# Moving work across the seam between w_out and the MLP of a transformer block

## The chip, the cores and the metric

The kernel runs on one core of a Trainium2 chip, as one launch. The metric is the device time of the whole launch in microseconds (us), the median of several runs; lower is better.

## The reference

One transformer block in float32, for 512 tokens and a width of 2048. A first half mixes two attentions (`nsa_attention` and `retention`) and projects the mix with `w_out`; a second half is an MLP of width 8192 with a squared relu. Each half is normalised before and after:

```
mix = concatenate([o_a, o_r], axis=-1) @ w_out[l]      # (512, 2048) @ (2048, 2048)
x = x + rms_norm(mix, norm_mix_post[l])
h = rms_norm(x, norm_mlp_pre[l])
u = square(relu(h @ w_up[l]))                          # (512, 2048) @ (2048, 8192)
x = x + rms_norm(u @ w_down[l], norm_mlp_post[l])      # (512, 8192) @ (8192, 2048)
```

## The kernel before, in words

**Splits.** Every float32 operand of a matmul is split into a high part (a cast to fp32r on ScalarE: `whi`, `Hh`) and a low part (the rest, a subtract on VectorE: `wlo`, `Hl`). A product of two such operands is three matmuls into the same PSUM tile, high by high, low by high, high by low (`mm3`, L154 to L156). So each piece of weight costs a load from HBM (asked for by SyncE), a cast, a subtract, and then matmuls. The tiles `whi` and `wlo` of the MLP lie in a pool of three buffers each, `hilo`.

**w_out.** Its 2048 columns are done in four blocks of 416 and a last block of 384 ("ends"). The first four are driven slab by slab (a slab is 256 rows of weight) by `drv.run`. The eight slabs of the last block, `wend[0..7]`, are loaded, cast and subtracted in a loop that alternates with the last steps of the fourth block: a step, then a slab's load. Their raw and split tiles lie in space that is given back at the end of this part. The last block then goes token tile by token tile: four tiles of 128 tokens, each 8 slabs x 6 matmuls. When a tile's columns are done, `mix_done` squares and sums them on ScalarE (L823) and scales them into `Y` on VectorE (L824).

**From w_out to the MLP.** Per token tile t, `x1_chain(t)` forms the norm's factor (a `pow` on GpSimd, L161), adds the residual `x` quarter by quarter (VectorE L1002; the x tile comes from HBM by `x_fetch`, and the next tile's quarter is asked for as soon as this one's is used), squares it on ScalarE (L1005), stores it (L1009) and forms the second norm's factor. `x1_out(t)` scales `Y` into `xh` (ScalarE L1022), transposes it on TensorE into the PSUM tile `PT` (L1035), multiplies by the gain back into `Y` (VectorE L1037) and splits it into `Hh`, `Hl` (`halves`: L143 and L144). Both are generators, cut into pieces by `yield`. `norm_pieces(t)` weaves the pieces of the chain of tile t with those of the output of tile t−1 in a written order. `beside(mainly, every, work)` takes a piece of `work` after every so many steps of the matmuls of `mainly`. The last tiles' pieces, and the sums of row quarters that the MLP needs (`x1_sums`, L1052 and L1060), are taken beside the first MLP products by `work3`, with a rate `due`.

**The up projection.** It works in 16 blocks of 512 hidden columns with a Strassen-like scheme of seven products (p = 0 to 6) per block, each with its own sum of weight quarters (11, 12, 21, 22) and sum of activation quarters. A product has two slabs of 24 matmuls of 128x256. `ADD` says which quarter is added to which (L949 on VectorE, or for product 3 by a DMA from GpSimd that accumulates on the way in, `late_sum`, L916), `SPLIT` which quarter is then split. Products 0 and 1 of blocks 0 to 3 and product 0 of block 4 need only the first two token tiles; they are done first ("early"). Then the blocks follow as 0, 4, 1, 5, 2, 6, 3, 7, 8 and so on, each in the order (0, 1, 2, 5, 4, 3, 6) of what is left. Blocks 1, 2 and 3 so have five products.

`up_done` combines the products into hidden values after each one; its tail after product 6 is four sums on VectorE (L1180 to L1183).

**Feed.** The class `Feed` runs ahead of the matmuls: `load` asks for a 1 MB quarter (two slabs) on SyncE (L923) whenever a slot is free, `advance` does a slab's add and cast (L949, L953) and then the subtract of the slab before it (`low`, L929); it keeps three slabs ahead. A slot comes free when the last subtract that reads its quarter has been issued. The slots are two parts of `low`, three lent tiles `pre` and later two rows of `Y`; the third part of `low` holds x. Each engine runs its own instructions strictly in program order.

Of the kernel before, what the change touches and what calls it, by code (L numbers as in the profile page):

```python
# [10 lines left out]
F32 = mybir.dt.float32  # L11
# [5 lines left out]
P = 128  # L17
S = 512
# [94 lines left out]
def block_kernel(ctx: ExitStack, tc: tile.TileContext, x, norm_mix_pre, w_in, cmp_pe_k, cmp_w1_k, cmp_b1_k,  # L113
# [738 lines left out]
    wend = slabs_of(w_out, [(NB * WB, LAST)], pool_r)  # L852
    for s in range(NSLAB):
        drv.run(16 * B + s + 1)
        wend[s].load()
    wctx.close()
# [11 lines left out]
    ptp = ctx.enter_context(tc.tile_pool(name="ptp", bufs=2, space=PS, side="right"))  # L868
    pr0 = ctx.enter_context(tc.tile_pool(name="pr0", bufs=1, space=PS, side="right"))
    hp = ctx.enter_context(tc.tile_pool(name="hilo", bufs=3, side="right", reuse_waits="tile"))  # L870
    rw = ctx.enter_context(tc.tile_pool(name="raws", bufs=1, side="right", reuse_waits="tile"))
    low = rw.tile([P, 6144], F32, name="low")
    xh = mp.tile([P, 2048], F32, name="xh")
# [12 lines left out]
    class Feed:  # L886
# [4 lines left out]

        def __init__(self, phases, slots, ahead):
            self.phases, self.free, self.ahead, self.lent = phases, list(slots), ahead, []
            self.n, self.at, self.R, self.ready = 0, 0, {}, {}
            self.loads, self.last = [], {}
            for i, (g, prod, source) in enumerate(phases):
                for q in (SPLIT[prod],) if self.by_dma(i) else (ADD[prod] or ()) + (SPLIT[prod],):
                    if (g, q) not in self.last:
                        self.loads.append((g, q, source, i))
                    self.last[g, q] = i  # L900
            self.held = None

        def by_dma(self, i):

            g, prod, _ = self.phases[i]
            return prod == 3

# [9 lines left out]

        def load(self):
            while self.loads and self.free and self.loads[0][3] <= self.n // 2 + self.ahead:
                g, q, source, _ = self.loads.pop(0)  # L920
# [18 lines left out]
        def advance(self):  # L939
# [10 lines left out]
            src = self.R[g, SPLIT[prod]][:, c]  # L950
            hi = hp.tile([P, SL], F32R, name="whi")
            lo = hp.tile([P, SL], F32R, name="wlo")
            nc.scalar.copy(hi, src)  # L953
# [33 lines left out]

    xt = [low[:, c:c + 512] for c in range(4096, 6144, 512)]

# [24 lines left out]
    def x1_out(t):  # L1014
# [16 lines left out]
        for q in range(4):  # L1031
# [6 lines left out]
            scaled(q + 2)  # L1038
            if q == 1 and t < 2:
                halves(0)  # L1040
            if q == 3:
                halves(8)
            yield

    def x1_sums(pair):
# [33 lines left out]

    def norm_pieces(t):  # L1080

        c = x1_chain(t) if t < NT else iter(())
        o = x1_out(t - 1) if t else iter(())
        for work in (o, o, o, o, o, c, c, c, c) if t == 2 else (c, o, c, c, o, o, c, o, o):
            if next(work, "end") != "end":
                yield
# [15 lines left out]
    phases = [((b, p), p, up_source(b)) for b, p in early]  # L1102
    phases += [(b, p, up_source(b)) for b in blocks for p in ORDER if (b, p) not in early]
    nup = len(phases)
# [9 lines left out]
    phases += [(("down", c, nb), p, dn_source(c, nb)) for c in range(NCH) for nb in range(2) for p in ORDER]  # L1114
    feed = Feed(phases, [low[:, 0:2048], low[:, 2048:4096]], 3)
    x5 = mp.tile([P, 512], F32, name="x5")
    tmp = Ring(*xt, *(xh[:, c:c + 512] for c in range(0, 2048, 512)), x5)
    state = [{} for _ in range(NBLK)]
# [8 lines left out]
    def up_done(b, p, ps):  # L1127
# [9 lines left out]
        if p == 0:  # L1137
            z["p0"] = tmp.take()
            nc.scalar.copy(v2(z["p0"]), ps)
# [4 lines left out]
        elif p == 2:  # L1144
            if b == 0:
                tmp.views = [Y[:, t, c:c + 512] for t in (1, 3) for c in range(0, 2048, 512)]
            elif b == NPRO:
                tmp.views += xt[:2]
            elif b == NPRO + 1:
                tmp.views += xt[2:] + [x5]  # L1150
            z["v"] = tmp.take()
# [59 lines left out]
    def primed():  # L1211
        for _ in range(2):
            feed.advance()
            yield

    for q in range(4):
        x_fetch(0, q)
    beside(ends[0][1](), 3, primed())
    beside(ends[1][1](), 1, norm_pieces(0))
    beside(ends[2][1](), 1, norm_pieces(1))  # L1220
    beside(ends[3][1](), 1, norm_pieces(2))
    rsctx.close()
# [3 lines left out]
    pr1 = ctx.enter_context(tc.tile_pool(name="pr1", bufs=2, space=PS))  # L1226
    pools = (pr1, pr0, pr1)
    sxv = [sxp.tile([P, 8, 2 * P], F32R, name=f"sx{i}") for i in range(2)]
    prctx = ExitStack()
    prp = prctx.enter_context(tc.tile_pool(name="prim", bufs=1, reuse_waits="tile"))  # L1230
    feed.lent = [prp.tile([P, 2048], F32, name=f"pre{i}") for i in range(3)]
    feed.free += feed.lent
    XA = [tuple(H[:, 0:8, 0:256] for H in (Hh, Hl)), tuple(H[:, 8:16, 0:256] for H in (Hh, Hl)),
# [21 lines left out]
    def work3():  # L1255
        yield from norm_pieces(3)
        yield from both(x1_sums(0), norm_pieces(4))
        feed.free += [Y[:, 0, :], Y[:, 2, :]]
        yield from x1_sums(1)
# [3 lines left out]
    for n, _ in enumerate(up(0, len(early), pools, XA)):  # L1263
        due += 1 if n < 9 else 0.6
        while due >= 1:
# [18 lines left out]

    g4 = low[:, 4096:6144]

# [132 lines left out]
```

## Time and profile before

| | us |
|---|---|
| runs shown, median (lowest to highest) | 2258.95 (2256.57 to 2261.75) |
| the profiled execution | 2263.74 |
| its span, first to last instruction | 2261.9 |
| TensorE busy | 2175.6 |
| VectorE busy | 1563.7 |
| ScalarE busy | 986.9 |
| mean granted TensorE clock | 0.989 |

w_out's last block starts at 900.32 us of the span, the MLP's first product at 946.98, and the down projection follows the up projection at about 1590. The page divides the span into 40 slices; a stage is read from the windows and timelines of that stage, not from the means over the span.

### The profile page before, as it was taken

The page shows a single profiled execution, that of the slowest core. Times are in us where ns is not written, and L with a number is a line of the kernel's source. Part 1 is how long each engine was busy: PE and PEld are TensorE (multiplying, and loading weights), DVE is VectorE, ACT ScalarE, POOL GpSimd, SP SyncE. Part 2 cuts the span into 40 slices and gives each one's busy share as a digit, 9 for nine tenths or more (in the row PEclk, how much of TensorE's full clock was granted, in tenths as well). Part 3 has the DMA queues.
Part 4 walks back from the last instruction along what each step waited for, and adds up shares of the span by engine and source line. Part 5 has one row for each costly group of instructions (what it writes and reads, how often), then busy time and mean ns, then how long its engine had stood idle before and what let it go on. Part 6 is the DMA issues. An engine that isn't in the chain of part 4 may idle for free.

```text
span 2261.9 us, 31774 instructions
## 1 busy us (share of the span) xinstructions
PE 2175.6 (96%) x12787; PEld 1919.0 (85%) x12787; DVE 1563.7 (69%) x1868; ACT 986.9 (44%) x1432; POOL 129.1 (6%) x147
## 2 busy tenths in 40 slices
PE   8999999999999999889999999999899999999994
PEld 7888878878787999889999999999778888888873
DVE  6223556554656623587777878787778998899897
ACT  5213343342232323564554555555654444444442
POOL 0000000000000000100000000000000000000002
PEclk9999999999999999999999999999999999999997
DMA  6543224322324334675876767666665656566655
GB/s 191 140 118 91 79 73 95 90 75 87 89 70 145 95 106 127 205 213 169 223 204 178 203 168 206 168 208 187 202 208 160 212 159 214 152 205 165 192 144 83
DMA packets 251989, 344.76 MB, mean 152 GB/s; under 512 B 14107, under 2 KB 163947, under 8 KB 251201
## 3 DMA queue, kind: packets, MB, share of 16 engines
q1 hardware_dynamic: 212000, 288.23, 39.4%
q0 software_dynamic: 29744, 42.96, 12.0%
q10 hardware_dynamic: 10098, 11.55, 1.5%
q8 instruction: 100, 1.64, 0.3%
q14 instruction: 47, 0.39, 0.1%
HBM read 300.95 MB, written 41.75 MB: 152 GB/s over the span
## 4 chain that ended last, share of the span: by engine, by line
PE 77%; DVE 12%; DMA 4%; ACT 3%; issue 3%; POOL 1%; SPq 0%; ACTq 0%; POOLq 0%; DVEq 0%
PE prod L155 13%; PE prod L156 13%; PE prod L154 13%; PE mm L154 11%; PE mm L156 10%; PE mm L155 10%; DVE wlo L929 4%; DMA Y<-in_w_up 2%; DVE Hl L144 2%; PE S L583 2%; ACT whi L953 1%; DVE low L949 1%; DVE Y L949 1%; DVE acc L1315 1%; DMA low<-in_w_up 1%
## 5 line engine op out<-in xcount | busy, mean ns | idle before, releaser
L953 ACT CAST whi<-Y 128x1024 fp32r<-128x1024 f32 x228 | 238.4, 1049 | 305.8 <-DVE Y L949 119.0
L155 PE MATMUL prod<-wlo,Hh 128*128 128x512 f32 x896 | 352.3, 393 | 18.3 <-DVE wlo L929 18.3
L156 PE MATMUL prod<-whi,Hl 128*128 128x512 f32 x896 | 349.0, 390 | 0.0
L154 PE MATMUL prod<-whi,Hh 128*128 128x512 f32 x896 | 348.7, 389 | 0.0
L953 ACT CAST whi<-low 128x1024 fp32r<-128x1024 f32 x214 | 224.3, 1052 | 282.2 <-DVE low L949 105.9
L144 DVE TENSOR_TENSOR wlo<-raw,whi 128x1024 fp32r<-128x1024 f32 (+4 forms) x152 | 168.6, 1113 | 255.9 <-ACT whi L143 255.4
L929 DVE TENSOR_TENSOR wlo<-Y,whi 128x1024 fp32r<-128x1024 f32 x228 | 277.6, 1222 | 61.6 <-ACT whi L953 59.9
L929 DVE TENSOR_TENSOR wlo<-low,whi 128x1024 fp32r<-128x1024 f32 x214 | 260.8, 1222 | 54.4 <-ACT whi L953 52.7
L156 PE MATMUL prod<-Hh,wlo 128*128 128x256 f32 x1024 | 286.2, 279 | 11.2 <-DVE wlo L929 11.2
L154 PE MATMUL prod<-Hh,whi 128*128 128x256 f32 x1024 | 285.7, 279 | 5.1 <-DVE Y L824 5.1
L155 PE MATMUL prod<-Hl,whi 128*128 128x256 f32 x1024 | 284.7, 278 | 0.0
L143 ACT CAST whi<-raw 128x1024 fp32r<-128x1024 f32 (+4 forms) x152 | 145.4, 960 | 302.5 <-PE mm L155 147.9
L154 PE MATMUL mm<-whi,Hh 128*128 128x416 f32 (+4 forms) x704 | 263.3, 374 | 0.5 <-ACT Hh L143 0.4
L156 PE MATMUL mm<-whi,Hl 128*128 128x416 f32 (+4 forms) x704 | 248.6, 353 | 0.6 <-DVE Hl L144 0.5
L155 PE MATMUL mm<-wlo,Hh 128*128 128x416 f32 (+4 forms) x704 | 248.1, 352 | 0.0
L155 PEld LDWEIGHTS prod<-wlo,Hh 128*128 128x128 f32 x896 | 168.1, 188 | 65.5 <-DVE wlo L929 31.0
L156 PE MATMUL prod<-sx,wlo 128*128 128x256 f32 x768 | 215.1, 280 | 8.1 <-DVE wlo L929 8.1
L154 PE MATMUL prod<-sx,whi 128*128 128x256 f32 x768 | 214.7, 280 | 0.5 <-ACT whi L953 0.5
L154 PE MATMUL mm<-Hh,whi 128*128 128x512 f32 x512 | 214.7, 419 | 0.1
L155 PE MATMUL prod<-sx,whi 128*128 128x256 f32 x768 | 214.5, 279 | 0.0
L156 PEld LDWEIGHTS prod<-Hh,wlo 128*128 128x128 f32 x1024 | 194.3, 190 | 13.6 <-DVE wlo L929 13.4
L156 PE MATMUL mm<-Hh,wlo 128*128 128x512 f32 x512 | 200.5, 392 | 0.0
(289 smaller groups left out, 3970.4 us busy)
## 6 DMA issues: line engine op xcount, KB each, us to landing
raw<-in_w_in SPq DMA_DIRECT2D x160, 256.0 KB, 3.1
low<-in_w_up SPq DMA_DIRECT2D x38, 1024.0 KB, 6.2
Y<-in_w_up SPq DMA_DIRECT2D x32, 1024.0 KB, 6.1
low<-in_w_down SPq DMA_DIRECT2D x32, 1024.0 KB, 5.2
Y<-in_w_down SPq DMA_DIRECT2D x32, 1024.0 KB, 5.2
Y<-ud SPq DMA_DIRECT2D x49, 512.0 KB, 8.4
ud<-Y SPq DMA_DIRECT2D x73, 256.0 KB, 4.7
raw<-in_w_out SPq DMA_DIRECT2D x32, 416.0 KB, 3.5
```

Of the source, the lines that this page charges most:

```text
L143: nc.scalar.copy(hi, src)
L144: nc.vector.tensor_sub(lo, src, hi.bitcast(F32))
L154: nc.tensor.matmul(ps, ah, bh, start=first, stop=False)
L155: nc.tensor.matmul(ps, ah, bl, start=False, stop=False)
L156: nc.tensor.matmul(ps, al, bh, start=False, stop=last)
L583: nc.tensor.matmul(sps[:, :c + L], QT[g][:, h, qs], k, start=True, stop=True)
L929: nc.vector.tensor_sub(lo, src, hi.bitcast(F32))
L949: nc.vector.tensor_add(to, to, by)
L953: nc.scalar.copy(hi, src)
L1315: nc.vector.tensor_add(e[p], ps, e[p])
```

## The change

1. The loop over the last block's slabs: each `wend` slab is loaded and split before the step of the fourth block beside it, not after it.
2. Space: the pool `raws` is allocated before `hilo` and holds three tiles, `low1`, `xrow`, `low0`, in place of one `low`. So they overlap other tiles of the w_out part than before. A small tile `x5` is dropped.
3. Loads: `low0` is asked for before the first x tile, `low1` right after it. `primed` splits three slabs of MLP weights, not two, beside the first token tile.
4. Pieces: halves are pieces of their own, and the written orders are new. `ends[1]` has the chain of tile 0 alone beside it. `pieces` replaces `norm_pieces`. The first product uses the PSUM tile `pr0`, the next ones `pr1`.
5. Blocks 1, 2 and 3 do their five products in the order (5, 2, 4, 3, 6), and blocks 0 to 3 (`short`) do the sum of product 3 on VectorE, not by the accumulating DMA.
6. The second slab of product 6 of each up block uses `whi` and `wlo` views that start 40 elements (160 B) into their tile.

```diff
     for s in range(NSLAB):
+        wend[s].load()
         drv.run(16 * B + s + 1)
-        wend[s].load()
...
+    rw = ctx.enter_context(tc.tile_pool(name="raws", bufs=1, side="right", reuse_waits="tile"))
+    low1, xrow, low0 = (rw.tile([P, 2048], F32, name=n) for n in ("low1", "xrow", "low0"))
     hp = ctx.enter_context(tc.tile_pool(name="hilo", bufs=3, side="right", reuse_waits="tile"))
-    rw = ctx.enter_context(tc.tile_pool(name="raws", bufs=1, side="right", reuse_waits="tile"))
-    low = rw.tile([P, 6144], F32, name="low")
...
-            return prod == 3
+            return prod == 3 and g not in self.short
...
-        def load(self):
-            while self.loads and self.free and self.loads[0][3] <= self.n // 2 + self.ahead:
+        def load(self, most=99):
+            while most and self.loads and self.free and self.loads[0][3] <= self.n // 2 + self.ahead:
+                most -= 1
...
-            hi = hp.tile([P, SL], F32R, name="whi")
-            lo = hp.tile([P, SL], F32R, name="wlo")
+            o = 40 if isinstance(g, int) and prod == 6 and s else 0
+            hi = hp.tile([P, SL + 128], F32R, name="whi")[:, o:o + SL]
+            lo = hp.tile([P, SL + 128], F32R, name="wlo")[:, o:o + SL]
...
-            if q == 1 and t < 2:
-                halves(0)
-            if q == 3:
-                halves(8)
             yield
+            if q % 2 and (q == 3 or t < 2):
+                halves(4 * (q - 1))
+                yield
...
-    def norm_pieces(t):
-
-        c = x1_chain(t) if t < NT else iter(())
-        o = x1_out(t - 1) if t else iter(())
-        for work in (o, o, o, o, o, c, c, c, c) if t == 2 else (c, o, c, c, o, o, c, o, o):
-            if next(work, "end") != "end":
+    def pieces(order, **works):
+
+        works = {k: iter(w) for k, w in works.items()}
+        for k in order:
+            if next(works[k], "end") != "end":
                 yield
...
-    phases += [(b, p, up_source(b)) for b in blocks for p in ORDER if (b, p) not in early]
+    phases += [(b, p, up_source(b)) for b in blocks for p in ((5, 2, 4, 3, 6) if 0 < b < NPRO else ORDER)
+               if (b, p) not in early]
...
+    feed = Feed(phases, [low0, low1], 3, range(NPRO))
...
     def primed():
-        for _ in range(2):
+        for _ in range(3):
             feed.advance()
             yield
-
+        feed.low()
+        yield
+
+    feed.load(1)
     for q in range(4):
         x_fetch(0, q)
-    beside(ends[0][1](), 3, primed())
-    beside(ends[1][1](), 1, norm_pieces(0))
-    beside(ends[2][1](), 1, norm_pieces(1))
-    beside(ends[3][1](), 1, norm_pieces(2))
+    feed.load(1)
+    outs = [x1_out(t) for t in range(NT)]
+    beside(ends[0][1](), 2, primed())
+    beside(ends[1][1](), 1, x1_chain(0))
+    beside(ends[2][1](), 1, pieces("accacaacaaa", a=outs[0], c=x1_chain(1)))
+    beside(ends[3][1](), 1, pieces("bccbcbbcbbb", a=outs[0], b=outs[1], c=x1_chain(2)))
...
-    pools = (pr1, pr0, pr1)
+    pools = (pr0, pr1, pr1)
...
-        yield from norm_pieces(3)
-        yield from both(x1_sums(0), norm_pieces(4))
+        yield from pieces("addadaadaa", a=outs[2], d=x1_chain(3))
+        yield from both(x1_sums(0), outs[3])
...
-        due += 1 if n < 9 else 0.6
+        due += 1 if n < 10 else 0.7
```

How the change moves the instructions is read from the order in which each engine has them. First SyncE at the seam, before. The last `raw` are w_out's last slabs, `low` and `pre` are slots of MLP weights, and four rows of `in_x` are one token tile:

```order
L175 DMA raw<-in_w_out 128x2x384 x3
L992 DMA low<-in_x 128x512 x4
L923 DMA low<-in_w_up 128x8x256 x2
L992 DMA low<-in_x 128x512 x12
L923 DMA pre_7473<-in_w_up 128x8x256
L923 DMA pre_7474<-in_w_up 128x8x256
L923 DMA pre_7475<-in_w_up 128x8x256
L923 DMA low<-in_w_up 128x8x256 x2
```

And in the changed kernel, where `low_7099` is `low0`, `low_7097` is `low1`, and x goes to `xrow`:

```order
L175 DMA raw<-in_w_out 128x2x384 x2
L925 DMA low_7099<-in_w_up 128x8x256
L995 DMA xrow<-in_x 128x512 x4
L925 DMA low_7097<-in_w_up 128x8x256
L995 DMA xrow<-in_x 128x512 x12
L925 DMA pre_7479<-in_w_up 128x8x256
L925 DMA pre_7480<-in_w_up 128x8x256
L925 DMA pre_7481<-in_w_up 128x8x256
L925 DMA low_7099<-in_w_up 128x8x256
L925 DMA low_7097<-in_w_up 128x8x256
```

One weight load now stands before the first x tile and one between it and the other three tiles' x.

ScalarE at the seam, before; the first two rows end the fourth block, L143 is the cast of w_out's last slab, L953 that of MLP weights, and the next L823 is token tile 0 of the last block:

```order
L823 ACTIVATE jk,st_5590<-mm 128x416
L823 ACTIVATE jk,st_5591<-mm 128x416
L143 CAST whi<-raw 128x768
L953 CAST whi<-low 128x1024 x2
L823 ACTIVATE jk,st_5588<-mm 128x384
L1005 ACTIVATE jk,st_5588<-Y 128x512 x4
L1009 DMA out<-Y 128x2048
```

And in the changed kernel, whose L956 and L1008 are the L953 and L1005 of before:

```order
L823 ACTIVATE jk,st_5590<-mm 128x416
L823 ACTIVATE jk,st_5591<-mm 128x416
L956 CAST whi<-low_7099 128x1024 x2
L956 CAST whi<-low_7097 128x1024
L823 ACTIVATE jk,st_5588<-mm 128x384
L1008 ACTIVATE jk,st_5588<-Y 128x512 x4
L1012 DMA out<-Y 128x2048
```

The cast of w_out's last slab has gone from between the two (it stands earlier), and three casts of MLP weights, the third of them of `low1`, stand ahead of tile 0's square sum.

VectorE where block 1 begins, before. L949 is a weight sum, L929 a low part, L1175 and L1180 to L1183 the end of the block before it; the two `wlo<-low` are product 2, the next two `wlo<-Y` product 5:

```order
L949 TENSOR_TENSOR low<-low,Y 128x1024
L929 TENSOR_TENSOR wlo<-low,whi 128x1024 x2
L1175 TENSOR_TENSOR Y<-prod,Y 128x512
L929 TENSOR_TENSOR wlo<-Y,whi 128x1024
L1180 TENSOR_TENSOR Y<-Y 128x512
L1181 TENSOR_TENSOR Y<-Y 128x512
L1182 TENSOR_TENSOR Y<-Y 128x512
L1183 TENSOR_TENSOR Y<-Y 128x512
L949 TENSOR_TENSOR low<-low,Y 128x1024
L929 TENSOR_TENSOR wlo<-Y,whi 128x1024
```

And in the changed kernel, whose L931, L951 and L1181 to L1184 are those rows' lines; here the two `wlo<-low_7097` are product 5, and the two `wlo<-Y` that follow are product 2:

```order
L931 TENSOR_TENSOR wlo<-low_7097,whi 128x1024
L951 TENSOR_TENSOR Y<-Y,low_7099 128x1024
L931 TENSOR_TENSOR wlo<-low_7097,whi 128x1024
L1176 TENSOR_TENSOR Y<-prod,Y 128x512
L951 TENSOR_TENSOR Y<-Y,low_7099 128x1024
L931 TENSOR_TENSOR wlo<-Y,whi 128x1024
L1181 TENSOR_TENSOR Y<-Y 128x512
L1182 TENSOR_TENSOR Y<-Y 128x512
L1183 TENSOR_TENSOR Y<-Y 128x512
L1184 TENSOR_TENSOR Y<-Y 128x512
L951 TENSOR_TENSOR Y<-Y,low_7097 128x1024
L931 TENSOR_TENSOR wlo<-Y,whi 128x1024
```

The four sums stood between the two slabs of product 5 and stand now between those of product 2, where an add of product 4 stands with them.

## Rows read from the trace of the kernel before

**Rows 1.** Page, span and busy time: us (share of span) and instructions.

```profile
span 2261.9 us, 31774 instructions
...
PE 2175.6 (96%) x12787; PEld 1919.0 (85%) x12787; DVE 1563.7 (69%) x1868; ACT 986.9 (44%) x1432; POOL 129.1 (6%) x147
```

**Rows 2.** Windows: stretch in us, length, busy us (instructions) by engine, clock, DMA share, GB/s.

```profile
925.70:946.70 21.00, 12.23 (x76) 10.97 (x74) 12.68 (x21) 11.00 (x20) 1.10 (x2) 0.97 0.28 104
946.70:952.20 5.50, 5.22 (x24) 5.22 (x25) 4.35 (x9) 3.47 (x7) 2.59 (x2) 0.50 0.65 215
1016.00:1040.00 24.00, 24.00 (x206) 24.00 (x205) 16.36 (x16) 12.07 (x15) 0.00 (x0) 1.00 0.49 144
1074.10:1102.80 28.70, 24.52 (x195) 23.73 (x194) 21.48 (x23) 13.16 (x16) 1.26 (x1) 0.94 0.84 230
1218.00:1245.70 27.70, 24.30 (x196) 23.71 (x195) 21.40 (x23) 13.19 (x17) 1.28 (x1) 0.94 0.87 238
1254.00:1278.00 24.00, 24.00 (x215) 24.00 (x214) 19.39 (x19) 12.08 (x14) 2.54 (x2) 1.00 0.65 171
1254.00:1588.00 334.00, 334.00 (x2950) 334.00 (x2949) 271.10 (x272) 183.79 (x224) 22.92 (x18) 1.00 0.68 190
```

**Rows 3.** Timeline, TensorE at the junction: start, us, instruction, [idle before <-releaser].

```profile
900.32 0.33 PE L154 MATMUL mm<-whi,Hh 128*128 128x384 f32 x1
...
904.30 0.34 PE L156 MATMUL mm<-whi,Hl 128*128 128x384 f32 x1
...
927.24 0.94 PE L1035 MATMUL PT<-misc,xh 128*128 128x128 f32 x5 [0.90 <-ACT xh L1022]
...
933.66 0.66 PE L1035 MATMUL PT<-misc,xh 128*128 128x128 f32 x4 [3.07 <-ACT xh L1022]
...
946.98 0.58 PE L154 MATMUL prod<-Hh,whi 128*128 128x256 f32 x1 [5.08 <-DVE Y L824]
```

**Rows 4.** Timelines of SyncE, ScalarE and VectorE at the junction.

```profile
889.05 0.37 SPq L175 DMA_DIRECT2D raw<-in_w_out  x1
...
902.36 1.68 SPq L923 DMA_DIRECT2D low<-in_w_up  x2
...
901.09 0.82 ACT L143 CAST whi<-raw 128x768 fp32r<-128x768 f32 x1
911.96 2.00 ACT L953 CAST whi<-low 128x1024 fp32r<-128x1024 f32 x2 [10.05 <-DMA low<-in_w_up]
913.86 0.48 ACT L823 ACTIVATE jk<-mm 128x384 f32<-128x384 f32 x1
...
915.96 2.74 DVE L1002 SCALAR_TENSOR_TENSOR Y<-Y,st,low 128x512 f32<-128x512 f32 x4 [0.68 <-POOL st L161]
...
925.00 0.75 DVE L1002 SCALAR_TENSOR_TENSOR Y<-Y,st,low 128x512 f32<-128x512 f32 x1 [1.01 <-DMA low<-in_x]
```

**Rows 5.** Waits of TensorE, 947 to 1015 us: us in total, times, longest.

```profile
PE prod L156 <- DVE wlo L929: 6.4, 5, 2.1
```

**Rows 6.** Timeline, TensorE in block 1: its longest stop.

```profile
1087.96 0.38 PE L156 MATMUL prod<-sx,wlo 128*128 128x256 f32 x1 [1.99 <-DVE wlo L929]
```

**Rows 7.** Timeline, VectorE in block 1.

```profile
1081.69 1.23 DVE L929 TENSOR_TENSOR wlo<-Y,whi 128x1024 fp32r<-128x1024 f32 x1 [4.15 <-ACT whi L953]
1082.88 0.69 DVE L1180 TENSOR_TENSOR Y<-Y 128x512 f32<-128x512 f32 x1
...
1085.55 1.22 DVE L949 TENSOR_TENSOR low<-low,Y 128x1024 f32<-128x1024 f32 x1
1086.69 1.22 DVE L929 TENSOR_TENSOR wlo<-Y,whi 128x1024 fp32r<-128x1024 f32 x1
```

**Rows 8.** Chain of waits in block 1 (start, us, what); then GpSimd's timeline.

```profile
1063.22 5.80 DMA Y<-in_w_up
...
1071.51 9.03 DMA Y<-in_w_up
...
1070.88 1.26 POOL L916 DMA_DIRECT2D Y<-in_w_up  x1 [24.04 <-DVE low L949]
```

More of the change, by code (lines that the diff above doesn't have):

```diff
@@ L886, in block_kernel, with __init__ @@
     class Feed:
-        def __init__(self, phases, slots, ahead):
+        def __init__(self, phases, slots, ahead, short):
             self.phases, self.free, self.ahead, self.lent = phases, list(slots), ahead, []
+            self.short = short
             self.n, self.at, self.R, self.ready = 0, 0, {}, {}
@@ L985, in block_kernel @@
     later = Later()
-    xt = [low[:, c:c + 512] for c in range(4096, 6144, 512)]
+    xt = [xrow[:, c:c + 512] for c in range(0, 2048, 512)]
     def x_fetch(t, q):
@@ L1114, in block_kernel @@
     phases += [(("down", c, nb), p, dn_source(c, nb)) for c in range(NCH) for nb in range(2) for p in ORDER]
-    feed = Feed(phases, [low[:, 0:2048], low[:, 2048:4096]], 3)
-    x5 = mp.tile([P, 512], F32, name="x5")
-    tmp = Ring(*xt, *(xh[:, c:c + 512] for c in range(0, 2048, 512)), x5)
+    feed = Feed(phases, [low0, low1], 3, range(NPRO))
+    tmp = Ring(*xt, *(xh[:, c:c + 512] for c in range(0, 2048, 512)))
     state = [{} for _ in range(NBLK)]
@@ L1137, in up_done @@
         if p == 0:
-            z["p0"] = tmp.take()
+            z["p0"] = fp.tile([P, S], F32, name="p0", tag="jk") if b == NPRO else tmp.take()
             nc.scalar.copy(v2(z["p0"]), ps)
@@ L1149, in up_done @@
             elif b == NPRO + 1:
-                tmp.views += xt[2:] + [x5]
+                tmp.views += xt[2:]
             z["v"] = tmp.take()
@@ L1231, in block_kernel @@
     feed.lent = [prp.tile([P, 2048], F32, name=f"pre{i}") for i in range(3)]
-    feed.free += feed.lent
+    feed.free = feed.lent + feed.free
     XA = [tuple(H[:, 0:8, 0:256] for H in (Hh, Hl)), tuple(H[:, 8:16, 0:256] for H in (Hh, Hl)),
@@ L1283, in u_operand @@
         later.add(3, lambda: split(ua[p][0], ua[p][1], r))
-    g4 = low[:, 4096:6144]
+    g4 = xrow
     def cols(nb, j):
```

## Prediction

> **What bounds the kernel now.** I began with the page's busy table: TensorE works 2175.6 of 2261.9 us [rows 1]. So an edit to another engine pays only where TensorE stands still or runs at its lower clock. The 40 slices put those places in the middle, around 900 to 1250 us, and the table by windows sizes them [rows 2]. In the undisturbed stretch 1254 to 1588 us one 128x256 matmul takes 334.00/2950 = 0.1132 us; a slab of 24 is 2.72 us. Against that:
>
> - 925.7 to 946.7 us, where w_out ends: 12.23 us busy of 21.00.
> - 946.7 to 952.2 us, the first MLP slab: 24 matmuls in 5.5 us at a granted clock of 0.50, the lower level (1.2 GHz), right after the longest stop.
> - Blocks 1, 2 and 3 of the up projection: three windows alike, of which the first and last are shown, each with about 4 us idle and a mean clock of 0.94.
>
> What TensorE waits for comes from its timeline. At the junction it stops for xh twice (0.90 and 3.07 us) and for Y once (5.08) [rows 3]. The timelines of ScalarE, VectorE and SyncE show why [rows 4]. SyncE asks for the first MLP weights only at 902.36, after x. ScalarE's two casts of them wait 10.05 us for that transfer and run at 911.96; the square sum of token tile 0 (L823) is queued behind them and starts at 913.86. TensorE finished tile 0 far sooner: its matmuls are (904.30 − 900.32)/23 = 0.173 us apart [rows 3], 48 of them end at 908.6. Everything after is late by that: residual at 915.96, norm, transposes, halves, first product. Within the MLP's first slabs five more stops of 6.4 us together wait for wlo [rows 5].
>
> In block 1 TensorE stops for wlo, the longest time before 1087.96, for 1.99 us [rows 6]. VectorE was itself held from about 1077.5 to 1081.69 by a cast whose weights were in flight, and then had four block sums, an add and a subtract before that wlo [rows 7]. The chain has the same: the transfer asked for at 1063.22 takes 5.80 us, the one at 1071.51 takes 9.03, with GpSimd's accumulating transfer issued at 1070.88 beside it [rows 8].
>
> **The change part by part.**
>
> *Junction* (last w_out slab split sooner, weights asked for before x, pieces by urgency, the first product in its own PSUM bank). The cast of the last w_out slab at 901.09 [rows 4] moves before the last drain of w_out's block, some 10 us sooner; it hides beside TensorE's matmuls. The last part of w_out is asked for at 889.05 now; loaded and cast a step sooner, its space is free by about 891 (an estimate), and the first weights go out then, x right behind. Even at the 9.6 us that the weights took from 902.36 to the cast at 911.96 [rows 4], both are there by 902. The second half (low1) lies where split weights of w_out lie, so it can start only when TensorE leaves them, at 900.3; at 5.8 to 9.0 us a transfer [rows 8] it lands at 906 to 909. ScalarE's cast of it still stands ahead of tile 0's square sum: from 907 to 910 at the latest, against TensorE's 908.6. I count with the square sum at 909, not 913.86; each us that low1 lands after 907.5 takes one from this. One VectorE subtract (1.22) stands before the residual, which comes at about 912.5, not 915.96: 3.5 us sooner, and from there tile 1 no longer shares its turn with tile 0's second half.
>
> What remains of the three stops (0.90 + 3.07 + 5.08 = 9.05 us [rows 3])? Transposes of tile 1 still meet scalings queued behind casts: I leave 1.5 us. The first product needs the first halves of tile 1: multiply 0.69, cast 1.00, subtract 1.23 after the second group of transposes = 2.9 us, against two groups of transposes of 0.66 that TensorE still has = 1.3: a wait of 1.6. So 3.1 us stay and 6.0 go. The lower clock in the first slab costs 5.5 − 2.72 = 2.8 us; it came after a stop of 5 us, which shrinks to under 2, and I give it three chances in four to go: 2.0. Together 8.0. The added wait is on low1: SyncE's x loads of tile 1 and the three pre loads are queued behind it, but they are wanted only from 912 on. In the early products two more pieces of row sums come before one wlo, on a VectorE that is nearly full (five stops [rows 5]): I take 0.5 off. Junction: **7.5 us**. Ends: 9.05 + 2.8 = 11.9 at best; at worst 0, if another piece becomes the last link, and below nothing one more residual wait such as the 1.01 us at 925.00 [rows 4], so −1.
>
> *Blocks 1 to 3* (order 5, 2, 4, 3, 6; product 3's sum on VectorE). By count, the block 1 window holds 195 matmuls: 28.7 − 195 × 0.1132 = 6.6 us lost; the last one 27.7 − 196 × 0.1132 = 5.5; three blocks at the mean of 6.07 lose 18.2. Of each, 28.7 × (1 − 0.94) = 1.7 is the lower clock and the rest stops.
>
> Removed: the transfer of the accumulate, so the load beside it comes nearer 5.80 than 9.03 [rows 8]; product 5 now comes before product 2 and its quarter is asked for where the other was, so the 4 us hold of VectorE goes. Added: two adds of 1.22 us per block on VectorE. Its load in a block's 10 slabs is 18 operations at a pitch of 1.14 (1085.55 to 1086.69) and 10 at 0.67 (1082.88 to 1085.55, four) [rows 7]: 27.2 us of 27.2. So it is full and can hide nothing. Between the wlo of the first and the second slab of product 2 still stand four sums, an add and a subtract: 4 × 0.67 + 2 × 1.14 = 5.0 us, against a slab of 2.72. A stop of 5.0 − 2.72 = 2.3 us stays per block; without the chain of stops before it I expect the clock to hold. Gain: 18.2 − 3 × 2.3 = **11.3 us**. Ends: 18.2 at best; below nothing, if VectorE is the bound, the adds come on top: 3 × 2 × 1.14 = 6.8 us lost. I take 11.3, since the load and the accumulates that made the hold are in rows and the sums that remain too. Block 0 has no earlier block whose four sums fall into its slabs, so VectorE has 4 × 0.67 = 2.7 us of room there for the two adds of 2.3: nothing.
>
> *The 160 B.* 16 slabs of 24 matmuls use tiles that start 160 B later. No row shows what a start address does. The rows show two paces at full clock: 206 matmuls in 24 us from 1016 on and 215 from 1254 on [rows 2], 116.5 and 111.6 ns, a difference of 4.9 ns. For 384 matmuls that is 1.9 us either way. I take 0: the later blocks already run at the faster pace. The Trainium skill says that TensorE's two reads of SBUF are independent and that loading weights takes nothing from a running matmul (page "TensorE: Matmul & The Clock Gate", section "Step-by-step: what each phase is for"), and that it never waits for another engine there ("SBUF — State Buffer", "Who interferes with whom"). By that this edit is worth 0 and there would be one pace; the trace, with 116.5 and 111.6 ns at a clock of 1.00, doesn't agree on the second point.
>
> *Sum*: 7.5 + 11.3 + 0 = 18.8 us. The profiled execution took 2263.74 us (span 2261.9 and 1.8 around it), so 2244.9; it stands 4.8 above the median of the runs, 2258.95, from which I subtract: **2240 us**.
>
> **The rivals.**
>
> *Blocks stay bound by VectorE.* For: 27.2 of 27.2 us. Then the two adds eat what the hold gave back, the stops keep throwing the clock, and only the junction pays: 2259 − 7.5 = 2251.5. Against: VectorE idled over 4 us per block before.
>
> *Nearly all goes.* Junction 11.9 and blocks 18.2, if a stop's wlo slides under earlier slack: 2259 − 30 = 2229. Against: the four sums stand where they stood.
>
> *The weights hold up x.* 1 MB now stands before x and the chain of tile 1 is paced by x (1.01 us wait at 925.00): the junction gives 0, the blocks 11.3: 2248.
>
> *Slower.* The pace locks. TensorE fell into 116.5 ns after a disturbance and left it after a stop [rows 2]; with fewer stops, or because of the moved slab at each block's end, it could enter the slower pace in block 0 and keep it for the whole up stage: 5376 matmuls × 4.9 ns = 26 us lost against 18.8 gained: 2266. It decides once more than 18.8/26, about 70%, of the stage runs so. For: both paces exist and last. Against: block after block from 1254 on kept the faster one.
>
> **How the numbers follow.** Forecast 0.52 (2235 to 2247), blocks bound by VectorE 0.17, nearly all goes 0.16, x late 0.07, slower 0.08. The range must leave out no more than two in ten: down to 2228 it holds most of "nearly all", up to 2254 all but the slower side. 0.2% of the time, 4.5 us, is about what a measurement here can tell from nothing. Faster by more: the first four cases but a few hundredths of the mild ones, 0.86; within: 0.06; slower: 0.08.
>
> **What would show it.** ScalarE's L823 of tile 0 starting by about 909 and not behind a cast that waits for weights. The first product about 6 us sooner relative to w_out's last block, and its first slab at full clock. In blocks 1 to 3 no GpSimd accumulate, no hold of VectorE on a cast, one stop of about 2.3 us at product 2's second slab, a clock of 1.00. The late up stage at 0.113 us a matmul. I am wrong if the first product still waits 5 us for Y, if a block's window still shows a mean clock of 0.94, or if the later blocks' pace changes.

## The result and the profile after

The changed kernel takes 2248.3 us, the median of five executions (2245.36 to 2251.03), against 2258.95 for the kernel before (2256.57 to 2262.2): 10.65 us less, a ratio of 0.9949 with a 95% interval of 0.9935 to 0.9964. The forecast was 2240 us with a range of 2228 to 2254. So the sign is right, the time lies in the range, and 11 of the 19 forecast microseconds came. The profiled execution after took 2248.3 us, its span is 15.4 us shorter than that of before: 4.8 us of this are no gain, since the profiled execution of before stood that far above its median.

The page's first lines after; compare [rows 1]:

```profile
span 2246.5 us, 31779 instructions
...
PE 2172.6 (97%) x12787; PEld 1916.7 (85%) x12787; DVE 1570.2 (70%) x1876; ACT 987.3 (44%) x1432; POOL 118.0 (5%) x139
```

TensorE does the same instructions and stands still 12 us less. ScalarE's and VectorE's timelines at the seam after; compare [rows 4]:

```profile
904.24 1.05 ACT L956 CAST whi<-low 128x1024 fp32r<-128x1024 f32 x1 [2.77 <-DMA low<-in_w_up]
907.29 0.49 ACT L823 ACTIVATE jk<-mm 128x384 f32<-128x384 f32 x1 [2.01 <-PE mm L156]
...
910.53 2.74 DVE L1005 SCALAR_TENSOR_TENSOR Y<-Y,st,xrow 128x512 f32<-128x512 f32 x4 [0.68 <-POOL st L161]
```

Tile 0's square sum (907.29) no longer waits for a cast but for TensorE itself, and the residual is at 910.53, not 915.96. TensorE's stops in the changed kernel, from its timeline; the first three answer to [rows 3]:

```profile
936.08 0.65 PE L1038 MATMUL PT<-misc,xh 128*128 128x128 f32 x4 [0.76 <-ACT xh L1025]
...
937.01 0.38 PE L154 MATMUL prod<-Hh,whi 128*128 128x256 f32 x1 [0.28 <-ACT Hh L143]
...
938.27 0.58 PE L155 MATMUL prod<-Hl,whi 128*128 128x256 f32 x1 [0.88 <-DVE Hl L144]
...
996.42 0.58 PE L156 MATMUL prod<-Hh,wlo 128*128 128x256 f32 x1 [3.72 <-DVE wlo L931]
...
1067.90 0.39 PE L156 MATMUL prod<-sx,wlo 128*128 128x256 f32 x1 [0.87 <-DVE wlo L931]
...
1075.70 0.38 PE L156 MATMUL prod<-Hh,wlo 128*128 128x256 f32 x1 [1.92 <-DVE wlo L931]
```

The stops at the seam fell from 9.05 us to 1.92, and the first product came 10.0 us sooner (937.01, not 946.98), 1.6 of them from executions that differ ahead of w_out's last block. But the stop at 996.42 is longer than any before it, and blocks 1 to 3 keep two stops each, of which the last two rows are the first pair. Windows after (columns as in [rows 2]); the first is the first product, the second the stop at 996.42, the last block 3's second stop:

```profile
936.90:942.50 5.60, 4.61 (x25) 4.41 (x26) 4.36 (x8) 2.83 (x6) 0.55 (x1) 0.70 0.91 290
...
992.00:1000.50 8.50, 4.78 (x29) 4.58 (x29) 8.46 (x9) 4.40 (x5) 0.00 (x0) 0.80 0.43 128
...
1214.00:1217.70 3.70, 3.70 (x20) 3.70 (x21) 3.70 (x4) 1.32 (x2) 0.00 (x0) 0.56 0.00 0
```

In this execution the lower clock came back in all three places, though the stops at the seam are now a fifth of what they were.

Block 1 in the changed kernel, VectorE's timeline and then SyncE's; compare [rows 7]:

```profile
1056.36 2.50 DVE L931 TENSOR_TENSOR wlo<-low,whi 128x1024 fp32r<-128x1024 f32 x2
...
1065.49 1.23 DVE L951 TENSOR_TENSOR Y<-Y,low 128x1024 f32<-128x1024 f32 x1 [2.68 <-DMA low<-in_w_up]
1066.63 1.22 DVE L931 TENSOR_TENSOR wlo<-low,whi 128x1024 fp32r<-128x1024 f32 x1
...
1070.63 0.69 DVE L1181 TENSOR_TENSOR Y<-Y 128x512 f32<-128x512 f32 x1
...
1074.42 1.22 DVE L931 TENSOR_TENSOR wlo<-Y,whi 128x1024 fp32r<-128x1024 f32 x1
...
1058.89 0.37 SPq L925 DMA_DIRECT2D low<-in_w_up  x1
```

VectorE still stands, 2.68 us, now at the add of product 2. That add reads a quarter asked for at 1058.89, the moment the last subtract of block 4 (ended 1058.86) gave its slot back; it landed some 6.5 us later. The subtract queued behind the add (1066.63) is the one that TensorE waits for at 1067.90; then come the four sums, and the subtract at 1074.42 ends the second stop.

### The profile page after: what moved, and what is told of

The parts are those of the page before. It is cut to its first block, busy times and chain, and to the rows that moved or that the text cites. A ratio compares the mean times of both kernels' runs of the same rounds, so it can differ in the third digit from the quotient of the medians.

```text
span 2246.5 us, 31779 instructions
## 1 busy us (share of the span) xinstructions
PE 2172.6 (97%) x12787; PEld 1916.7 (85%) x12787; DVE 1570.2 (70%) x1876; ACT 987.3 (44%) x1432; POOL 118.0 (5%) x139
## 3 DMA queue, kind: packets, MB, share of 16 engines
q0 software_dynamic: 25520, 38.77, 10.9%
## 4 chain that ended last, share of the span: by engine, by line
PE 80%; DVE 12%; issue 3%; ACT 3%; DMA 2%; POOL 1%; SPq 0%; POOLq 0%; ACTq 0%; DVEq 0%
PE prod L155 14%; PE prod L156 14%; PE prod L154 13%; PE mm L154 11%; PE mm L156 11%; PE mm L155 11%; DVE wlo L931 4%; DVE Hl L144 2%; PE S L583 2%; DVE Y L951 1%; DVE low L951 1%; ACT whi L956 1%; DVE acc L1321 1%; PE S L706 1%; PE PT L646 1%
## 5 line engine op out<-in xcount | busy, mean ns | idle before, releaser
L956 ACT CAST whi<-low 128x1024 fp32r<-128x1024 f32 x230 | 241.8, 1052 | 287.3 <-DVE low L951 103.6
L956 ACT CAST whi<-Y 128x1024 fp32r<-128x1024 f32 x212 | 222.3, 1049 | 283.5 <-DVE Y L951 126.7
L931 DVE TENSOR_TENSOR wlo<-low,whi 128x1024 fp32r<-128x1024 f32 x230 | 280.0, 1220 | 48.1 <-ACT whi L956 46.3
L931 DVE TENSOR_TENSOR wlo<-Y,whi 128x1024 fp32r<-128x1024 f32 x212 | 257.8, 1221 | 36.6 <-ACT whi L956 35.0
L143 ACT CAST whi<-raw 128x1024 fp32r<-128x1024 f32 (+4 forms) x152 | 145.6, 960 | 301.4 <-PE mm L155 148.0
L154 PE MATMUL prod<-sx,whi 128*128 128x256 f32 x768 | 212.2, 276 | 0.0
L155 PE MATMUL prod<-sx,whi 128*128 128x256 f32 x768 | 212.2, 276 | 0.0
```

What stands on the lines that cost most here:

```text
L154: nc.tensor.matmul(ps, ah, bh, start=first, stop=False)
L155: nc.tensor.matmul(ps, ah, bl, start=False, stop=False)
L931: nc.vector.tensor_sub(lo, src, hi.bitcast(F32))
```

## The experiments

Each kernel ran on one chip beside the kernel before and the others of its group; a ratio with its interval is against all executions of before in the group. The executions of the kernel before fell in two groups of times, for a reason that the first group of experiments found, so the table lists them apart; where the lower one is compared, this is said. On the 2nd and 3rd chip the groups of before run into each other, and the table cuts them at 2262.

| kernel | executions | median us | lower group | upper group | ratio (95%) |
|---|---|---|---|---|---|
| before, 1st chip | 35 | 2271.4 | 15: 2254.5 to 2261.8 | 20: 2265.3 to 2276.1 | |
| e1_seam | 12 | 2251.3 | 9: 2247.9 to 2252.9 | 3: 2262.1 to 2265.9 | 0.9940 (0.9912 to 0.9969) |
| e2_blocks | 12 | 2263.4 | 6: 2255.0 to 2259.4 | 6: 2267.4 to 2273.8 | 1.0002 (0.9976 to 1.0029) |
| e3_no_move | 12 | 2250.4 | 7: 2245.7 to 2250.9 | 5: 2259.5 to 2262.4 | 0.9947 (0.9919 to 0.9974) |
| e4_sums_gpsimd | 12 | 2252.3 | 12: 2249.6 to 2255.5 | none | 0.9950 (0.9928 to 0.9971) |
| before, 2nd chip | 17 | 2263.3 | 8: 2255.0 to 2260.7 | 9: 2263.3 to 2274.4 | |
| f1_after_again | 6 | 2250.1 | 6: 2247.5 to 2251.4 | none | 0.9936 (0.9911 to 0.9962) |
| f2_before_move | 12 | 2260.8 | 12: 2258.0 to 2263.1 | none | 0.9985 (0.9968 to 1.0002) |
| f3_move_four | 6 | 2249.7 | 6: 2248.3 to 2250.4 | none | 0.9936 (0.9914 to 0.9959) |
| e5_sums_later | 6 | 2247.2 | 6: 2246.5 to 2248.3 | none | 0.9927 (0.9905 to 0.9950) |
| before, 3rd chip | 32 | 2262.0 | 16: 2251.3 to 2261.8 | 16: 2262.2 to 2277.0 | |
| g1_later_four | 12 | 2247.9 | 10: 2245.4 to 2250.2 | 2: 2259.8 to 2260.7 | 0.9931 (0.9905 to 0.9958) |
| g2_all_moved | 12 | 2273.2 | 12: 2270.3 to 2277.1 | none | 1.0041 (1.0017 to 1.0065) |
| e6_due | 12 | 2250.3 | 12: 2249.7 to 2251.7 | none | 0.9942 (0.9923 to 0.9962) |
| e7_order_only | 9 | 2248.0 | 9: 2245.3 to 2248.4 | none | 0.9930 (0.9905 to 0.9955) |

**The seam alone.** Taken out of the changed kernel: the order of blocks 1 to 3, the sum on VectorE, the 160 B.

```diff
-    phases += [(b, p, up_source(b)) for b in blocks for p in ((5, 2, 4, 3, 6) if 0 < b < NPRO else ORDER)
+    phases += [(b, p, up_source(b)) for b in blocks for p in ORDER
-    feed = Feed(phases, [low0, low1], 3, range(NPRO))
+    feed = Feed(phases, [low0, low1], 3, ())
-            o = 40 if isinstance(g, int) and prod == 6 and s else 0
+            o = 0
```

> The change without its part for the up blocks (order of products and the sum of product 3 as before) and without the 160 B. The profiles of before and after put the seam's gain at 9.8 us up to the first product that needs all four token tiles. Theory: the seam carries most of the change; the median lies 8 to 10 us under before, ratio 0.9955 to 0.9965. Rival: what the seam gives comes back as waits for wlo where the early products end (in the changed kernel a stop of 3.9 us and a stretch at the lower clock at 992 us); then the gain is 3 to 5 us, ratio about 0.998.

In the lower groups the medians are 2250.1 and 2258.9: the seam gives 8.8 us. Between the lower groups the theory holds. It is the gain of the seam's parts together (the loop over the slabs, the space, the loads, the pieces, the PSUM tile); no run separates them.

**The blocks alone**, put into the kernel before:

```diff
-            return prod == 3
+            return prod == 3 and g not in range(4)
-    phases += [(b, p, up_source(b)) for b in blocks for p in ORDER if (b, p) not in early]
+    phases += [(b, p, up_source(b)) for b in blocks for p in ((5, 2, 4, 3, 6) if 0 < b < NPRO else ORDER)
+               if (b, p) not in early]
```

> The kernel before with one part alone: products of blocks 1 to 3 in the order 5, 2, 4, 3, 6, and in blocks 0 to 3 the sum of product 3 on VectorE. Theory: about 3 us a block where the clock holds, 6 to 9 us in all, ratio 0.996 to 0.9975; in the trace each of the three blocks keeps two stops for wlo, of about 1.0 and 2.1 us, because VectorE stands about 2.7 us on the quarter that product 2's add reads and then does four block sums. Rival, the forecast's own: VectorE no longer stands at all and only the second stop is left, 11 us, ratio 0.995.

Lower groups: 2256.5 against 2258.9, 2.4 us, less than either expected; on top of the seam (e3 against e1) it is 1.5. The two stops are there as the theory said. The profiled execution took 2271.05 us, and its trace shows why there are two groups. A window in which neither kernel has a stop, of this kernel and then of e3_no_move:

```profile
1260.00:1500.00 240.00, 240.00 (x2040) 240.00 (x2039) 188.39 (x188) 127.91 (x158) 15.28 (x12) 1.00 0.65 180
```

```profile
1260.00:1500.00 240.00, 240.00 (x2120) 240.00 (x2119) 195.22 (x197) 133.64 (x165) 15.28 (x12) 1.00 0.66 185
```

TensorE is busy all through and granted its full clock in both, but does 2040 matmuls here and 2120 there: 117.6 and 113.2 ns. In the first the slower pace begins at 1245 us, with the first slab behind block 3, and lasts for 124 slabs, to the end of the up projection: 124 x 24 x 4.4 ns = 13.1 us. The medians of the two groups are 14.9 us apart here and 14.0 in the kernel before. Block 3's last stop ended 19 us earlier (1225.99), and the slabs between ran at 113 ns: no stop set the slower pace here.

**Without the 160 B** in the changed kernel:

```diff
-            o = 40 if isinstance(g, int) and prod == 6 and s else 0
+            o = 0
```

> The changed kernel with all split weights at the start of their tiles (no 160 B). Theory: the moved slab itself runs at 117 ns a matmul, not 113, so 0.08 us in each of 16 slabs is saved, 1.3 us, but in block 0 the slower pace of 118 ns, which in the changed kernel ends in the moved slab, lasts until a stop: between 1 us faster and 1 us slower, 2247 to 2250. Rival: without it the slower pace lasts through the later up blocks, whole blocks at 118 ns: 5 us or more slower, in some executions if not in all.

The rival was right, in 5 of 12 executions. The theory's part on the price isn't settled by times: the other seven have a median of 2248.6, and the changed kernel, on other chips, had 2250.1 (f1) and 2248.3 (the result). The trace settles it: the 16 moved slabs of the changed kernel run at 116 to 117 ns a matmul.

**The four sums on GpSimd** in blocks 4 to 6:

```diff
-                nc.vector.tensor_sub(s1, z["x"], z["v"])
+                e = nc.gpsimd if NPRO <= b < 2 * NPRO - 1 else nc.vector
+                e.tensor_tensor(s1, z["x"], z["v"], op=ALU.subtract)
...
```

> The changed kernel with the four sums that end blocks 4, 5 and 6 on GpSimd, not on VectorE. Theory: these four sums, which stand between the subtracts of product 2's two slabs, are what is left of the stops; without them the stop of 2.1 us in blocks 1, 2 and 3 goes and with it the stretch at the lower clock in block 3: 6 to 8 us faster than the changed kernel, about 2241. Rival: GpSimd's sums and VectorE's two-input operations get in each other's way, the VectorE rows beside them grow by about what was saved, and the time stays within 2 us of 2248.

The rival's mechanism holds, and the time is a little worse than it had it: 2252.3, 2.2 us over the changed kernel on another chip (f1). VectorE's timeline in block 1, then GpSimd's:

```profile
1070.19 1.22 DVE L931 TENSOR_TENSOR wlo<-Y,whi 128x1024 fp32r<-128x1024 f32 x1
1071.45 2.20 DVE L951 TENSOR_TENSOR Y<-Y,low 128x1024 f32<-128x1024 f32 x1
1073.57 2.31 DVE L931 TENSOR_TENSOR wlo<-Y,whi 128x1024 fp32r<-128x1024 f32 x1
...
1072.64 2.16 POOL L1183 TENSOR_TENSOR Y<-Y 128x512 f32<-128x512 f32 x1
```

The same add and subtract take 2.20 and 2.31 us beside GpSimd's sums, 1.22 alone. Four operations of VectorE grow so (the next two take 2.19 and 2.31), by 4.1 us together; the four sums had cost it 2.8.

**The changed kernel again.** No edit.

> The changed kernel once more, many times, on the chip of the three beside it. The kernel before fell into two groups of times in the last experiments, 2254 to 2262 and 2265 to 2276 us, and so did the kernels without the 160 B. Theory: the upper group is the slower pace (118 ns a matmul) kept from block 3 to the end of the up projection, about 124 slabs of 0.108 us = 13.4 us, and the moved slab ends it in each block: all times of this kernel lie within 2245 to 2253. Rival: the two groups come from elsewhere (the chip, the memory): this kernel too has executions at 2259 and above.

Six executions within 4 us, beside a kernel before that spread over 19.

**The 160 B alone**, in the kernel before (and `x5` dropped, with its two uses, and `p0` of block 4 in a tile of its own, as in the change):

```diff
-            hi = hp.tile([P, SL], F32R, name="whi")
-            lo = hp.tile([P, SL], F32R, name="wlo")
+            o = 40 if isinstance(g, int) and prod == 6 and s else 0
+            hi = hp.tile([P, SL + 128], F32R, name="whi")[:, o:o + SL]
+            lo = hp.tile([P, SL + 128], F32R, name="wlo")[:, o:o + SL]
```

> The kernel before with the 160 B alone; to make room for the longer tiles the small tile x5 is dropped as in the change. Theory: the lower group of times goes up by 16 x 0.08 = 1.3 us, to 2256 to 2263, and the upper group, 2270 to 2276, is gone; so its median lies over the lower group of before and under the upper one, by about 12 us. Rival: the slower pace ends by the shorter stops of the changed kernel, not by the moved slab; then both groups stay.

The theory holds: twelve executions, none above 2263.1. The median is 2.1 us over the lower group of before (2258.7); 1.3 were expected. It is not the longer tiles that end the upper group: e3_no_move has them, without the move, and has both groups.

**The 160 B in blocks 0 to 3 only**:

```diff
-            o = 40 if isinstance(g, int) and prod == 6 and s else 0
+            o = 40 if g in range(4) and prod == 6 and s else 0
```

> The changed kernel with the 160 B in blocks 0 to 3 only, where stops can throw the pace. Theory: the moved slab costs 0.08 us wherever it stands and helps only after a stop; the last stop of the up projection is in block 3, so 12 x 0.08 = 1 us is saved and no execution falls into the upper group: about 2247 to 2249. Rival: the slower pace can come back without a stop in blocks 8 to 15, and some executions lie 5 us or more higher.

0.5 us less than f1, within what six executions each can tell; no upper group in these six, but see g1.

**The four sums three slabs later**:

```diff
-            later.add(2, sums)
+            later.add(5 if NPRO <= b < 2 * NPRO - 1 else 2, sums)
```

> The changed kernel with the four sums of blocks 4, 5 and 6 on VectorE, three slabs later. On GpSimd they gained nothing: they took 2.0 to 2.3 us each and VectorE's operations beside them grew from 1.22 to 2.2 us. Theory: VectorE is full in these blocks, so the stop of 2.1 us moves to a later slab, split in smaller ones; the total changes by less than 2 us (2247 to 2250). Rival: the work just stands in the wrong place, and three slabs later it finds slack: 6 us faster, about 2242.

2.9 us under f1, between the two. TensorE's waits from 1060 to 1240 us, in the changed kernel first, then here (us in total, times, longest):

```profile
PE prod L156 <- DVE wlo L931: 8.5, 6, 1.9
```

```profile
PE prod L156 <- DVE wlo L931: 8.1, 10, 1.1
```

The total of the waits hardly changes, as the theory said, but no stop is over 1.1 us, and in this profile the clock stays at its full level from 1060 to 1250 us, where the changed kernel's two profiles have 0.99 and 0.98 (one stretch and two at the lower level). At 1.7 us a stretch, the price that the prediction read from a block of before, that is an estimate of 1.7 to 3.4 us, which would cover the gain.

**Both together**: the later sums and the 160 B in blocks 0 to 3.

> The changed kernel with the sums of blocks 4 to 6 three slabs later and the 160 B in blocks 0 to 3 only. The later sums alone ran at 2247.2 beside 2250.1 of the changed kernel, the 160 B in four blocks at 2249.65. Theory: the two add: 3 us and up to 1 us, 2246 to 2247, all in one group. Rival: the moved slabs of blocks 8 to 15 were needed and some executions lie over 2255.

Ten executions are as the theory had them; two are at 2259.8 and 2260.7, so the rival is right in these. That the slower pace came back behind the last moved slab would explain them, and e4_sums_gpsimd shows that it can: there it begins behind block 1's moved slab, without a stop, and lasts until block 5's moved slab. Of g1's two executions no trace was taken. The first of two windows of e4 lies between those two moved slabs, the second in the block behind block 2's, at 113 ns:

```profile
1098.00:1134.00 36.00, 36.00 (x308) 36.00 (x307) 28.72 (x30) 18.46 (x23) 2.55 (x2) 1.00 0.64 176
1169.50:1199.50 30.00, 30.00 (x267) 30.00 (x266) 25.10 (x26) 15.23 (x18) 2.54 (x2) 1.00 0.71 192
```

Both counts hold two or three matmuls that the ends of the window cut; the starts are 118 and 113 ns apart.

**Every slab moved**, up and down:

```diff
-            o = 40 if isinstance(g, int) and prod == 6 and s else 0
+            o = 40
```

> The changed kernel with every slab of the MLP's split weights 160 B into its tile, up and down. It asks whether the start address itself sets the pace or its change from one slab to the next. Theory: the start address sets it, a slab that starts there runs at 117 ns: 224 up slabs x 0.08 = 18 us less the 1.3 already paid, about 2265, in one group. Rival: what counts is the change between slabs; then all slabs run at 113 or 118 ns as without the move and there are two groups again, near 2249 and 2262.

One group: the start address itself counts, not its change from slab to slab. Two windows, one of the up and one of the down projection, here and then without the move (e3_no_move):

```profile
1260.00:1500.00 240.00, 240.00 (x2059) 240.00 (x2059) 189.27 (x189) 129.36 (x159) 15.29 (x12) 1.00 0.64 180
1700.00:1800.00 100.00, 100.00 (x427) 79.95 (x426) 88.38 (x76) 43.29 (x42) 4.75 (x4) 1.00 0.59 179
```

```profile
1700.00:1800.00 100.00, 99.52 (x437) 81.38 (x435) 88.95 (x77) 44.22 (x43) 7.12 (x6) 1.00 0.64 189
```

240 us / 2059 = 116.6 ns in the up projection, where 113 and 118 are the two paces without a move. The expectation left the down projection out of its sum; there too it is slower (427 matmuls against 437). From its first matmul to its last it takes 648.0 us here (from 1592.9) and 637.5 in e3 (from 1579.1), 10.5 us more; with the expected 2265 that would make 2275.5, and 2273.2 were measured.

**The old rate of pieces**:

```diff
-        due += 1 if n < 10 else 0.7
+        due += 1 if n < 10 else 0.6
```

> The changed kernel with the rate of the pieces beside the early products back at 0.6 from the tenth on (0.7 in the change). Theory: VectorE is full from 980 to 1000 us, so the stop of 3.9 us before the last early slab splits into one of about 1.7 there and one of about 2.2 in the slab behind it, as before the change; the time stays within 1 us of the changed kernel, 2249 to 2251. Rival: the two pieces that come too soon are the cause, and the stop shrinks without coming back: 2 to 3 us faster.

As the theory has it: the same time (f1, the changed kernel on another chip, had 2250.1). TensorE's waits from 975 to 1012 us, in the changed kernel and then here:

```profile
PE prod L156 <- DVE wlo L931: 4.9, 2, 3.7
```

```profile
PE prod L156 <- DVE wlo L931: 6.7, 4, 2.8
```

One long stop becomes several shorter ones, with more in total, 6.7 us against 4.9.

**The order alone**, product 3's sum by the accumulating transfer again:

```diff
-    feed = Feed(phases, [low0, low1], 3, range(NPRO))
+    feed = Feed(phases, [low0, low1], 3, ())
```

> The changed kernel with the sum of product 3 done by GpSimd's accumulating transfer in all blocks, as before; the order 5, 2, 4, 3, 6 of blocks 1 to 3 stays. Theory: the two stops that are left in each of these blocks (1.0 and 2.1 us) come before product 3, from the quarter that lands late and from the four sums, so the way of its sum doesn't touch them: within 1.5 us of the changed kernel. Rival, the forecast's: the accumulates beside the loads hold the loads up, and without the VectorE sum the blocks lose 3 us each: 2258.

Its nine executions have a median of 2248.0, 2.4 us under e6 on the same chip and 2.2 under f1 on another: with the new order the sum on VectorE gains nothing. The forecast's rival fails, and the theory's 1.5 us are passed on the other side: by these numbers the sum on VectorE costs some 2 us. The changed kernel itself wasn't run on that chip.

## Why the prediction was right or wrong

**The seam** was forecast at 7.5 us; the seam alone gives 8.8 in the lower groups. The mechanism is the one forecast: weights there before x, tile 0's sum at TensorE's pace. Of the 9.05 us of stops, 3.1 were to stay; 1.92 did. The lower clock in the first slab was to go with three chances in four; it stayed in the profiled execution (0.70 in the window after; 24 matmuls in 5.45 us), but not in f1's, the same kernel with the same stops in that slab (0.28 and 0.88 us; 3.99 us):

```profile
937.80:943.40 5.60, 4.65 (x38) 4.46 (x39) 4.40 (x8) 2.87 (x7) 0.55 (x1) 1.00 0.91 298
```

The profiles of e1, e4 and e7 have the full clock there too, those of e3, e5, e6, f3, g1 and g2 do not. So this term is a chance, as the forecast had it, but a smaller one: the full clock in four of eleven profiles. Half a microsecond was taken off for the fuller VectorE behind it, where the stop is 3.72 us. Before, four stops of 5.3 us stood there together, now two of 4.9.

**The blocks** were forecast at 11.3 us and gave 1.5 to 2.4. This is the step that failed, in two terms. First its base, 18.2 us lost: that was read from one execution. Windows from 1060 to 1250 us, of before and of the two other kernels with the old order there, e1_seam and f2_before_move:

```profile
1060.00:1250.00 190.00, 178.67 (x1510) 176.57 (x1509) 148.95 (x152) 95.42 (x118) 12.72 (x10) 0.97 0.70 192
```

```profile
1060.00:1250.00 190.00, 180.67 (x1523) 178.86 (x1522) 151.55 (x155) 97.71 (x121) 15.27 (x12) 0.98 0.74 204
```

```profile
1060.00:1250.00 190.00, 178.92 (x1529) 177.07 (x1528) 150.96 (x153) 96.99 (x121) 12.71 (x10) 0.99 0.71 196
```

The profile that the forecast used has the lower clock in all three blocks, the others in two and one: 5.1 us of the 18.2 were the dear side of something that comes and goes. The new order has it in one block (after) or two (f1), so only part of it was the change's to give. Second, the claim that VectorE's hold goes. The forecast saw that the quarter product 5 needs would be asked for sooner, and didn't ask which quarter takes its place as the last one: it is the one that product 2's add reads, and the slot that it waits for comes free with the same subtract as before. So the hold moved from a cast to an add, and fell from 4.15 to 2.68 us. The 2.3 us that were to stay at the second slab are there (1.92); the 0.87 before it were not expected. The waits for wlo between 1060 and 1250 us went from 10.9 us to 8.5.

**The 160 B** were forecast at 0, and the slower pace was a rival with 0.08, for the changed kernel. The slower pace is real, but it is the kernels without the move that keep it, and the moved slab ends it. In the traces of the kernels with the move, eleven moved slabs follow a slab at 118 ns (one in the changed kernel, one in f1, two each in e7, f2 and f3, three in e4); the slab behind runs at 113 in all eleven, without a wait. Where the last slab of a block isn't moved, 17 such slabs are at 118 (before, e1, e2, e3 and a block of f3): the slab behind stays at 118 in fifteen, and in the other two TensorE waits there. The moved slab costs 16 x 0.08 = 1.3 us in every execution, by its pace, and saves some 13 in those that would keep the slower pace to the end; on the later chips that was about half of before's executions, in the five of the result none. So the forecast's sum misses 1.3 us there. Its reason, that the later blocks run at the faster pace already, took one execution for all; its 4.9 ns between the paces are 4.4, since the ends of a window of 24 us count in 111.6, and its row for 334 us gives 113.2. The forecast drew from the Trainium skill (page "SBUF — State Buffer", section "Who interferes with whom": "PE and ACT never wait on anyone") that the edit is worth 0. No run here shows TensorE waiting for another engine in SBUF, so the sentence itself isn't contradicted; what was drawn from it is: with the start address alone changed, 113.2 ns became 116.6 at a granted clock of 1.00.

Together, 8.8 + 2 − 1.3 = 9.5 us, against 10.65 measured.

## What to carry to other kernels

A stage's loss read from one profile may include the clock's or the pace's dear side: look whether the same stage loses as much in another execution before it is put into a sum. When an order is changed so that a late operand is no longer late, name the operand that is last now, and which event frees its buffer; here it was the same one. Moving two-input work from a full VectorE to GpSimd gave nothing back, while spreading it over later slabs, with the total unchanged, was worth 2.9 us, and ten of g1's twelve executions, with the same sums, lie about as far under e6 on a third chip.

## What the runs showed of the hardware that was not expected

At full clock and without a wait, 128x256 matmuls run at 113 or at 118 ns, and in e2 the slower pace lasted for 350 us. A slab that starts 160 B later runs at about 116, and where no stop comes in, the pace behind it is 113 in every traced case but one (block 1 of e4). A stop is not needed to enter the slower pace or to leave it: it began in e2 (1245 us), e3 (1163) and e4 (1098) where one pair of starts lay 162, 169 and 220 ns apart, and ended in the kernel before (1043), where two pairs lay 270 and 222 ns apart; the prediction took it to end there after a stop. In the trace of the changed kernel, the slab before the move in block 0 and the one behind it, windows:

```profile
1016.00:1025.00 9.00, 9.00 (x79) 9.00 (x78) 6.88 (x8) 4.70 (x6) 0.00 (x0) 1.00 0.77 240
```

```profile
1028.80:1031.20 2.40, 2.40 (x24) 2.40 (x23) 0.81 (x1) 0.00 (x0) 0.00 (x0) 1.00 1.04 333
```

The second window is short, and 24 matmuls in 2.40 us counts its ends; the spacing of their starts there is 113 to 114 ns, and 117 to 119 in the first. Which addresses meet in this, no run here shows. What set two executions of g1_later_four back by 12 us is open too; e4 shows a way.

The fastest kernel that showed no upper group is the changed one with the sums of blocks 4 to 6 three slabs later, 2247.2 us; that with the order alone is 2248.0. The two together were not run.
